# Attention loads in another order and two gate outputs held until 1/rms is spread

## The chip, the cores and the metric

The kernel runs on one core of one Trainium2 chip. The metric is the device time of one execution in microseconds (us). The profile names the engines PE (TensorE matmul), PEld (its weight loads), DVE (VectorE), ACT (ScalarE), POOL (GpSimd) and SP (SyncE, which issues most DMAs).

## The reference

One layer of an encoder for 1024 tokens of width 1024. A combined input projection feeds two groups of heads, a bidirectional mLSTM and a neighbourhood attention over a grid of 16 rows by 64 columns; then come an output projection, an MLP and a gated embedding.

```python
def reference(x, p, norm1_g, w_in, ..., w_ple_gate, w_ple_up):
    u = rms_norm(h, norm1_g[i])
    proj = jnp.einsum('bsd,de->bse', u, w_in[i])
    y_a = mlstm_mixer(mq, mk, mv, mo, mg, ...)
    y_b = neighbourhood_attention(nq, nk, nv, q_norm_g[i], k_norm_g[i], rpb[i])
    h = h + jnp.einsum('bse,ed->bsd', jnp.concatenate([y_a, y_b], axis=-1), w_out[i])
    z = jnp.einsum('bsd,df->bsf', rms_norm(h, norm2_g[i]), w_ff1[i])
    h = h + jnp.einsum('bsf,fd->bsd', jnp.square(jax.nn.relu(z)), w_ff2[i])
    gate = jax.nn.sigmoid(jnp.einsum('bsd,de->bse', rms_norm(h, ple_norm_g[i]), w_ple_gate[i]))
    h = h + gate * jnp.einsum('bsk,kd->bsd', p[i], w_ple_up[i])
```

In the attention each query sees a window of 8 rows by 16 columns; a relative position bias, taken from `rpb`, is added to the scores before the softmax.

## The kernel before

Everything is held transposed, channels on the 128 partitions and the 1024 tokens along the free axis. Products run in three passes of split operands (`passes`: high by high, high by low, low by high). The stages follow each other: input projections, mLSTM by head (`mlstm_front`, `mlstm_sweeps`, `mlstm_finish`), attention with the output projection between its steps, the rest of the output projection, the MLP's two products, the gate.

**Attention.** 32 units n are handled in an order written out by hand (`with tc.manual_schedule()`): a pair of heads (`pr`, 4), a half of the grid (`rb`, 2), a block of columns (`cb`, 4; `KW` gives 24 or 32 key columns). In unit n, PE computes the scores of n+1 and the values (probabilities times `vw`) of n-1; DVE and ACT make the softmax of n+1 (`exps`, which adds the bias table `tab`), ACT and POOL normalise it (`norm`; POOL's half is L955), PE transposes the probabilities of n (`pt`, L966), and DVE and ACT copy them out (`pT`).

Between these steps other work is put. `run(nv1, k)` takes k steps of the last projection (24 matmuls each, evacuated by ACT into `nv1t` with three buffers and written to `nvd` by SP). `y_split` splits the mLSTM's output into a high and a low part. `fill(k)` takes k matmuls (`op`, L1014) of the output projection: six jobs (`JOBS`) of two output rows `e` each, three over the four mLSTM inputs (48 matmuls each), three over three attention inputs (36 each). `FILLA` and `FILLB` give k for each quarter of the 32 units. A job's weights are loaded by `w_raw` (buffers `wr`, three) and split by `w_split` on ACT and DVE; the sums are added to the rows `h` of x that `out_res` loads.

**Tables.** `tab_load(n)` fills a unit's table of 128 partitions: 64 from `tabI` through SP, 64 from `tabU` through POOL's queue, and a strip set to a constant on POOL. Five buffers (`TABS`) let the load of table n+5 start when the softmax of unit n has read its own. The source of each part is a list of dimensions whose outermost has 4 entries:

```python
for q_, tb, p0, r0, c0, nr in ((nc.sync, tabI, io, 0, 0, 12), (nc.gpsimd, tabU, bo, r_0, a0, 8)):
    src = bass.AP(tb.tensor, tb.offset + k0 * 30 * kw + r0 * 2 * kw,
                  [[2 * kw, 4], [30 * kw, 16], [1, nr * 2 * kw]])
```

`load_vw(pr)` loads the values of a pair of heads in four DMAs, one for each `cb`, from `nvd[:, columns, pr]`, whose outermost dimension also has 4 entries. SP issues its DMAs in the order of its list, and each waits for what its buffer waits for. The pool `m2`, which holds tables, values and probabilities, opens when the mLSTM's pool `m1` closes.

**Gate.** For each of eight rows e and two halves t of the tokens `g_unit(e, t)` makes 24 matmuls into a PSUM tile; `g_out` multiplies by 1/rms (`Rb`), takes the sigmoid, multiplies by the embedding and adds. For the first row (e = 0) the sum of squares is finished on PE (`n_1ps`, `n_0ps`), DVE and POOL (`sumsq_to_rstd`; POOL takes the power), and PE transposes and ACT copies spread it (`bcast_rstd`; `n_1R`, `n_0R`). This stage's order is not written out by hand.

Of the kernel before, what the change touches and what calls it, by code (L numbers as in the profile page):

```python
# [11 lines left out]
F32 = mybir.dt.float32  # L12
# [6 lines left out]
P = 128  # L19
# [16 lines left out]
TABS = 5  # L36
PCS = 5
FILLA = (4, 4, 3, 7)
FILLB = (4, 4, 3, 7)
# [5 lines left out]
NEG = -1.0e30  # L45
# [13 lines left out]
def tile_block(ctx, tc, xT, pT, w_in, w_out, w_ff1, w_ff2, w_gate, w_up, vecs, gate_b, rpbp, con,  # L59
               outT, dbg=None):  # L60
    nc = tc.nc
# [617 lines left out]
    aa, MP, wpv, wj, enm = (gk[n] for n in ("aa", "MP", "wpv", "wj", "enm"))  # L679
    m1p_ctx = tc.tile_pool(name="m1p", bufs=1, space=PSUM)  # L680
    m1p = m1p_ctx.__enter__()
    with tc.tile_pool(name="m1", bufs=2) as m1:
# [185 lines left out]
        for h in range(4):  # L868
            mlstm_sweeps(h)
            if h == 0:  # L870
                na_ssq(7)
            if h < 3:
                mlstm_front2(h + 1)
                run(o0) if h == 0 else run(o1, 5) if h == 1 else run(o1)
            if h < 2:
                mlstm_front(h + 2)
            if h == 2:
                nv1 = proj_nv(1)
        run(nv1, NV1)
# [9 lines left out]
    with tc.tile_pool(name="m2", bufs=2) as m2, tc.tile_pool(name="m2p", bufs=2, space=PSUM) as m2p:  # L889
# [10 lines left out]
        NU = 32  # L900
        g3 = lambda t_: t_.rearrange("p (r c) -> p r c", c=64)
        heads2 = (slice(0, 64), slice(64, 128))
        tabs, scs, sms, pts, pvs, vws, ys = {}, {}, {}, {}, {}, {}, {}

        def geom(n):
            pr, u = divmod(n, 8)
            rb, cb = divmod(u, 4)
            return pr, rb, cb, KW[cb], 12 * KW[cb]

        def tab_load(n):  # L910
            if n >= NU:
                return
            pr, rb, cb, kw, w_ = geom(n)
            tab = m2.tile([P, 12, 2, 32], F32, tag="tab", name=f"tab{n}", bufs=TABS)
            tab = tab.rearrange("p a s b -> p (a s b)")[:, : 2 * w_]
            io, bo = (0, 64) if rb == 0 else (64, 0)
            r_0, a0, dead = (4, 0, 8) if rb == 0 else (0, 4, 0)
            k0 = (64 if cb > 1 else 0) + 16 * pr
            for q_, tb, p0, r0, c0, nr in ((nc.sync, tabI, io, 0, 0, 12), (nc.gpsimd, tabU, bo, r_0, a0, 8)):
                tb = tb[min(cb, 3 - cb)]  # L920
                src = bass.AP(tb.tensor, tb.offset + k0 * 30 * kw + r0 * 2 * kw,
                              [[2 * kw, 4], [30 * kw, 16], [1, nr * 2 * kw]])
                q_.dma_start(tab[p0 : p0 + 64, c0 * 2 * kw : (c0 + nr) * 2 * kw], src)
            G.memset(tab[bo : bo + 64, dead * 2 * kw : (dead + 4) * 2 * kw], NEG)
            tabs[n] = tab.rearrange("p (a s b) -> p s a b", s=2, b=kw)
# [119 lines left out]
        raws, ws_ = {}, {}  # L1045

        def fill_jobs():
            for i, (es, ks) in enumerate(JOBS):
                if i + 1 < len(JOBS):
                    raws[i + 1] = w_raw(*JOBS[i + 1])  # L1050
                n = 0
                while len(yhi) <= ks[-1]:
                    yield
                for _ in out_proj(es, ks, mmps, ws_.pop(i)):
                    n += 1
                    if n == 12 and i + 1 < len(JOBS):
                        ws_[i + 1] = w_split(raws.pop(i + 1), *JOBS[i + 1])
                    yield

# [42 lines left out]
        with tc.manual_schedule():  # L1102
            for n in range(TABS):
                tab_load(n)
                if n == 1:
                    vws[0] = load_vw(0)
            raws[0] = w_raw(*JOBS[0])
# [5 lines left out]
            for n in range(NU):  # L1113
# [17 lines left out]
                if n < 4:  # L1131
                    run(nv1, 1 if n < 2 else None)
                    if n > 1:
                        y_split(2 * n - 4)
                else:
                    fill(FILLA[n // 8])
# [11 lines left out]
                if n < 4:  # L1148
                    run(nv1, 1) if n < 2 else None
                    if n > 1:  # L1150
                        y_split(2 * n - 3)
                    if n == 2:
                        ws_[0] = w_split(raws.pop(0), *JOBS[0])
                else:
                    fill(FILLB[n // 8])
                if n in (2, 3, 9):
                    e0 = {2: 0, 3: 2, 9: 4}[n]
                    out_res(e0)
                    out_res(e0 + 1)
# [3 lines left out]
            run(fills)  # L1163
# [170 lines left out]
    with tc.tile_pool(name="ff2", bufs=2) as ff2:  # L1334
# [143 lines left out]
        g_load(2)  # L1478
        for e, t in [(0, 1), (1, 1), (0, 0), (1, 0)] + [(e, t) for e in range(2, 8) for t in (1, 0)]:
            if (e, t) == (7, 0):  # L1480
                parts = [g_unit(e, t, q * 256, 256) for q in range(2)]
                for ps, cs in parts:
                    g_out(e, ps, cs, V)
                continue
            ps, cs = g_unit(e, t)
            if e == 0:
                rs3 = sumsq_to_rstd(acc3[t], hc[t], f"n3_{t}")
                bcast_rstd(rs3, hc[t], f"n3_{t}")
            g_out(e, ps, cs, G if t else V)
            if t == 0 and e + 2 < 8:  # L1490
                g_weights(e + 2)
                load_up(e + 2)
                if e + 3 < 8:
                    g_load(e + 3)
# [53 lines left out]
```

## Time and profile before

| | before |
|---|---|
| median of 3 runs | 1414.97 us (1414.75 to 1416.21) |
| profiled execution | 1421.5 us |
| span of its instructions | 1419.7 us |
| PE busy | 1316.8 us (93%) |
| DVE, ACT, POOL busy | 916.7, 592.8, 566.3 us |
| data moved by DMA | 206.06 MB, mean 145 GB/s |

The profile is of one execution. A row of the chain of waits gives the start, the length and what the last-ending chain of work spent it on; "DMA tab<-tabU" is the time from a DMA's issue to its landing. [...] A tile's buffer numbers are left out of its name.

### The profile page before, as it was taken

How to read it: one execution, taken by the hardware profiler on the slowest of the kernel's cores; microseconds unless marked ns; L12 is line 12 of the kernel's file. 1: busy time of each engine (PE TensorE's matmuls, PEld its weight loads, DVE VectorE, ACT ScalarE, POOL GpSimd, SP SyncE). 2: the span in 40 equal slices, each digit the busy share in tenths (PEclk: the TensorE clock that was granted, in tenths of full speed). 3: DMA queues.
4: the chain of work that ended last, by engine and by line, in shares of the span. 5: the costliest groups of instructions: out<-in, count | busy, mean ns of one | idle time of the engine just before them, and what ended most of it. 6: DMA issues, size and time to landing. Idle time of an engine off the chain costs nothing.

```text
span 1419.7 us, 19398 instructions
## 1 busy us (share of the span) xinstructions
PE 1316.8 (93%) x7115; PEld 1100.4 (78%) x7115; DVE 916.7 (65%) x1419; ACT 592.8 (42%) x971; POOL 566.3 (40%) x456
## 2 busy tenths in 40 slices
PE   7999999999987669997899999999999799999898
PEld 6888777899876447775678888888788578888787
DVE  4487897665662436669856666665638998568433
ACT  7453343455553435545333333323433334455321
POOL 2215675553431112206456555665203560026422
PEclk9999999999998789998899999999999999999999
DMA  8543333564325454411144444455876674452342
GB/s 277 206 145 96 107 119 105 175 216 153 105 72 146 140 138 102 133 45 45 31 163 151 146 153 135 150 163 188 296 261 224 190 227 124 151 155 62 92 138 82
DMA packets 155343, 206.06 MB, mean 145 GB/s; under 512 B 20848, under 2 KB 104880, under 8 KB 155248
## 3 DMA queue, kind: packets, MB, share of 16 engines
q1 hardware_dynamic: 142480, 182.10, 40.7%
q10 hardware_dynamic: 7200, 13.11, 2.8%
q0 software_dynamic: 5568, 9.61, 2.4%
q8 instruction: 56, 0.92, 0.3%
q14 instruction: 39, 0.32, 0.1%
HBM read 151.60 MB, written 53.17 MB: 144 GB/s over the span
## 4 chain that ended last, share of the span: by engine, by line
PE 62%; DVE 7%; DMA 6%; issue 4%; POOL 2%; ACT 1%; SPq 0%; DVEq 0%; POOLq 0%; ACTq 0%
PE f_P L1364 17%; PE p_s_t L255 9%; PE g L1433 6%; PE p L255 6%; PE op L1014 4%; PE p_s L255 3%; PE p_t L255 3%; PE o0p L309 2%; PE pv L986 2%; DMA wo_4r<-w_out 1%; PE o1p L309 1%; PE pt L966 1%; PE num L754 1%; PE sc L936 1%; DMA tab<-tabI 1%
## 5 line engine op out<-in xcount | busy, mean ns | idle before, releaser
L1253 DVE TENSOR_TENSOR zl<-zr,zh 128x1024 fp32r<-128x1024 f32 x56 | 82.4, 1479 | 6.3 <-ACT zh L1252 6.3
L255 PE MATMUL p<-b,w_ah 128*128 128x512 f32 x256 | 80.3, 396 | 3.5 <-DVE b L192 3.5
L955 POOL TENSOR_SCALAR pc<-pc,st 128x288 f32<-128x288 f32 (+1 forms) x32 | 17.2, 538 | 154.6 <-DVE st L950 94.8
L1234 POOL TENSOR_TENSOR w2re<-sk,w2re 128x512 f32<-128x512 f32 x16 | 27.0, 1686 | 100.1 <-issue 63.5
L259 DVE TENSOR_TENSOR z<-z,p_s_t 128x512 f32<-128x512 f32 x64 | 42.5, 685 | 33.0 <-PE p_s_t L255 31.7
L1252 ACT ACTIVATE zh<-zr 128x1024 fp32r<-128x1024 f32 x56 | 58.3, 1047 | 12.0 <-DMA zr<-zd 11.1
L255 PEld LDWEIGHTS p<-b,w_ah 128*128 128x128 f32 x256 | 48.9, 191 | 14.1 <-DVE b L192 3.9
L986 PE MATMUL pv<-pT,vw 128*64 128x128 f32 (+1 forms) x384 | 30.4, 295 | 31.7 <-DVE pT L975 31.7
L1364 PE MATMUL f_P<-zl,w2h 128*128 128x512 f32 x128 | 51.7, 404 | 8.2 <-DVE zl L1253 8.1
L255 PE MATMUL p<-b,w_al 128*128 128x512 f32 x128 | 50.8, 399 | 7.6 <-DVE w_al L140 7.6
L945 ACT ACTIVATE pc<-pc,st 128x288 f32<-128x288 f32 (+1 forms) x64 | 36.3, 569 | 48.7 <-DVE st L944 48.7
L944 DVE CUSTOM_DVE_ANT_1 pc<-sc,tab 128x288 f32<-128x288 f32 (+1 forms) x64 | 29.9, 504 | 40.2 <-POOL pc L955 12.6
L1387 POOL TENSOR_TENSOR h<-h,evP 128x512 f32<-128x512 f32 x8 | 14.8, 1886 | 98.3 <-ACT evP L1378 98.3
L1277 POOL TENSOR_TENSOR tz<-z,z 128x512 f32<-128x512 f32 x16 | 20.8, 1298 | 82.6 <-ACT z L1266 82.6
L986 PEld LDWEIGHTS pv<-pT,vw 128*64 128x64 f32 (+1 forms) x384 | 22.1, 144 | 39.1 <-DVE pT L975 33.1
L1433 PE MATMUL g<-gh,wg_l 128*128 128x512 f32 (+1 forms) x136 | 52.4, 386 | 0.0
L1433 PE MATMUL g<-gh,wg_h 128*128 128x512 f32 (+1 forms) x136 | 52.4, 385 | 0.0
L758 POOL TENSOR_SCALAR wv<-vh,wj 128x129 f32<-128x129 f32 x56 | 30.4, 546 | 54.6 <-PE num L759 49.5
L1433 PE MATMUL g<-gl,wg_h 128*128 128x512 f32 (+1 forms) x136 | 52.0, 382 | 0.0
L1364 PE MATMUL f_P<-zh,w2h 128*128 128x512 f32 x128 | 50.7, 396 | 1.2 <-ACT zh L1252 1.2
L1265 DVE SCALAR_TENSOR_TENSOR z<-z,Rb 128x1024 f32<-128x1024 f32 x32 | 50.5, 1582 | 0.9 <-ACT Rb L179 0.9
L1364 PE MATMUL f_P<-zh,w2l 128*128 128x512 f32 x128 | 50.6, 395 | 0.0
(698 smaller groups left out, 4607.4 us busy)
## 6 DMA issues: line engine op xcount, KB each, us to landing
zr<-zd SPq DMA_DIRECT2D x56, 512.0 KB
zd<-z ACTq DMA_DIRECT2D x48, 256.0 KB
w2r<-w_ff SPq DMA_DIRECT2D x48, 256.0 KB
w_0r<-w_ff SPq DMA_DIRECT2D x16, 512.0 KB
w_1r<-w_ff SPq DMA_DIRECT2D x16, 512.0 KB
zd<-tz SPq DMA_DIRECT2D x32, 256.0 KB
zd<-z SPq DMA_DIRECT2D x32, 256.0 KB
w2re<-w_ff SPq DMA_DIRECT2D x16, 512.0 KB
```

The source lines that it names most:

```text
L255: TE.matmul(ps, x_, y_, start=j == 0 and i == 0, stop=j == 3 and i == 2)
L259: mark["add"] = V.tensor_tensor(o, a, b, op=ALU.add).ins
L309: mm = TE.matmul(ps[:, :256], a, b, start=k == 0 and i == 0, stop=k == KT - 1 and i == 2)
L758: G.tensor_scalar(wv, vh[:, c, 0:129], wj[:, col], 1.0, op0=ALU.mult, op1=ALU.mult)
L945: S.activation(pb, pb, AF.Exp, scale=-1.0, bias=st[:, 0:1], accum_out=st[:, 1:2])
L986: TE.matmul(pv[e0 : e0 + 64, cb], vws[pr][: 4 * kw, cb, rb + j, e0 : e0 + 64], pT[s][: 4 * kw, j], start=j == 0, stop=j == 2)
L1014: TE.matmul(ps, a, b, start=n == 0 and i == 0, stop=n == len(ks) - 1 and i == 2)
L1252: S.activation(hi, raw, AF.Copy)
L1253: dv.append(V.tensor_tensor(lo, raw, hi.bitcast(F32), op=ALU.subtract).ins)
L1265: V.scalar_tensor_tensor(z_, z_, 0.0, Rb, op0=ALU.max, op1=ALU.mult)
L1364: pe_last = TE.matmul(ps[n, e], a, b, start=st and k == 0, stop=sp and k == 2)
L1433: TE.matmul(ps, x_, y_, start=k == 0 and i == 0, stop=k == KT - 1 and i == 2)
```

## The change

`tab0` gets a pool of its own with one buffer, opened ahead of the mLSTM's pools; every fifth table uses it, the others rotate over four buffers. Table 0 is loaded in the mLSTM stage. `tabU` is issued by SP. The last projection takes two, one, one and one steps in units 0 to 3; `y_split` comes once in each of units 3 to 6; the fills start with unit 7 (`NJ`) and take ten a unit at first. A job's weights are loaded when the job two ahead of it is being split (`job_weights`), the first three in units 1, 4 and 6; rows `h` come one a unit in units 4 to 7, 9 and 10. In the gate two outputs are collected in `held` until the transposes of 1/rms have been issued, and weights are loaded one row further ahead.

```diff
-FILLA = (4, 4, 3, 7)
-FILLB = (4, 4, 3, 7)
+FILLA = (5, 5, 4, 7)
+FILLB = (5, 5, 4, 7)
+NJ = 7
...
+    tb0_ctx = tc.tile_pool(name="tb0", bufs=1)
+    tb0 = tb0_ctx.__enter__()
     m1p_ctx = tc.tile_pool(name="m1p", bufs=1, space=PSUM)
...
+        pool, tag, bufs = tabp[0] if n % TABS else (tb0, "tab0", 1)
+        tab = pool.tile([P, 12, 2, 32], F32, tag=tag, name=f"tab{n}", bufs=bufs)
...
+        for q_, tb_, p0, r0, c0, nr in ((nc.sync, tabI, io, 0, 0, 12), (nc.sync, tabU, bo, r_0, a0, 8)):
...
             if h == 2:
                 nv1 = proj_nv(1)
+                tab_load(0)
...
+        tabp.append((m2, "tab", TABS - 1))
...
         def fill_jobs():
             for i, (es, ks) in enumerate(JOBS):
-                if i + 1 < len(JOBS):
-                    raws[i + 1] = w_raw(*JOBS[i + 1])
-                n = 0
                 while len(yhi) <= ks[-1]:
                     yield
+                done[0] = 0
                 for _ in out_proj(es, ks, mmps, ws_.pop(i)):
-                    n += 1
-                    if n == 12 and i + 1 < len(JOBS):
-                        ws_[i + 1] = w_split(raws.pop(i + 1), *JOBS[i + 1])
+                    done[0] += 1
                     yield
+                cur[0] += 1
+
+        def job_weights():
+
+            i = cur[0] + 1
+            if done[0] >= 12 and i in raws and i not in ws_:
+                ws_[i] = w_split(raws.pop(i), *JOBS[i])
+                if i + 2 < len(JOBS):
+                    raws[i + 2] = w_raw(*JOBS[i + 2])
...
-            for n in range(TABS):
+            for n in range(1, TABS):
+                if n == 2:
+                    vws[0] = load_vw(0)
                 tab_load(n)
-                if n == 1:
-                    vws[0] = load_vw(0)
-            raws[0] = w_raw(*JOBS[0])
...
                 if n < 4:
-                    run(nv1, 1 if n < 2 else None)
-                    if n > 1:
-                        y_split(2 * n - 4)
-                else:
+                    run(nv1, 1 if n < 3 else None)
+                if n >= NJ:
                     fill(FILLA[n // 8])
...
-                if n < 4:
-                    run(nv1, 1) if n < 2 else None
-                    if n > 1:
-                        y_split(2 * n - 3)
-                    if n == 2:
-                        ws_[0] = w_split(raws.pop(0), *JOBS[0])
-                else:
+                if n < 1:
+                    run(nv1, 1)
+                if n >= NJ:
                     fill(FILLB[n // 8])
-                if n in (2, 3, 9):
-                    e0 = {2: 0, 3: 2, 9: 4}[n]
-                    out_res(e0)
-                    out_res(e0 + 1)
+                if 3 <= n < 7:
+                    y_split(n - 3)
+                if n == 6:
+                    ws_[0] = w_split(raws.pop(0), *JOBS[0])
+                job_weights()
+                if n in (1, 4, 6):
+                    j = {1: 0, 4: 1, 6: 2}[n]
+                    raws[j] = w_raw(*JOBS[j])
+                if n in (4, 5, 6, 7, 9, 10):
+                    out_res({4: 0, 5: 1, 6: 2, 7: 3, 9: 4, 10: 5}[n])
...
         g_load(2)
+        g_load(3)
+        held = []
...
-            ps, cs = g_unit(e, t)
+            held.append((e, *g_unit(e, t), G if t else V))
             if e == 0:
                 rs3 = sumsq_to_rstd(acc3[t], hc[t], f"n3_{t}")
+                continue
+            if e == 1:
                 bcast_rstd(rs3, hc[t], f"n3_{t}")
-            g_out(e, ps, cs, G if t else V)
-            if t == 0 and e + 2 < 8:
+                if t == 0:
+                    g_weights(2)
+            while held:
+                g_out(*held.pop(0))
+            if e == 1 and t == 0:
+                load_up(2)
+                g_load(4)
+                g_weights(3)
+                load_up(3)
+                g_load(5)
+            elif t == 0 and e + 2 < 8:
                 g_weights(e + 2)
                 load_up(e + 2)
-                if e + 3 < 8:
-                    g_load(e + 3)
+                if e + 4 < 8:
+                    g_load(e + 4)
```

The order of the instructions shows it at three places. First the list of SP from table 5 on: `nv1t` are steps of the last projection, `nr` raw queries and keys, `vw1` the second set of values, `wo0_0r` the first job's weights. Before:

```order
L923 DMA tab4_4403<-tabI0_111 64x1x576
L1020 DMA wo0_0r_4407<-w_out 128x4x256
L923 DMA tab5_4445<-tabI1_112 64x1x768
L342 DMA nvd_81<-nv1t3_4474 128x2x128
L342 DMA nvd_81<-nv1t4_4518 128x2x128
L836 DMA nr3_4536<-qnd3_85 128x1024
L894 DMA vw1_4538<-nvd_81 96x1x512
L894 DMA vw1_4538<-nvd_81 128x1x512 x2
L894 DMA vw1_4538<-nvd_81 96x1x512
L923 DMA tab6_4551<-tabI1_112 64x1x768
```

and now:

```order
L708 DMA tab5_4446<-tabI1_112 64x1x768
L708 DMA tab5_4446<-tabU1_114 64x1x512
L343 DMA nvd_81<-nv1t3_4475 128x2x128
L343 DMA nvd_81<-nv1t4_4519 128x2x128
L866 DMA nr3_4537<-qnd3_85 128x1024
L925 DMA vw1_4539<-nvd_81 96x1x512
L925 DMA vw1_4539<-nvd_81 128x1x512 x2
L925 DMA vw1_4539<-nvd_81 96x1x512
L708 DMA tab6_4552<-tabI1_112 64x1x768
L708 DMA tab6_4552<-tabU1_114 64x1x512
L343 DMA nvd_81<-nv1t5_4581 128x2x128
L1029 DMA wo0_0r_4600<-w_out 128x4x256
```

Each table now has two rows in SP's list, and the first weights stand behind table 6 instead of ahead of table 5. Second, SP's list in the mLSTM stage, where `mq7` and `qw2_0` are loads of that stage. Before:

```order
L149 DMA nv1_0r_3957<-w_in 128x4x256
L690 DMA mq7_3571<-mqd7_105 128x1024
L334 DMA ogd_80<-o0t0_2926 128x256
L707 DMA qw2_0_3136<-Md_110 128x1024
L696 DMA vh2_3131<-vd_79 128x8x128
```

and now:

```order
L150 DMA nv1_0r_3960<-w_in 128x4x256
L708 DMA tab0_3972<-tabI0_111 64x1x576
L708 DMA tab0_3972<-tabU0_113 64x1x384
L720 DMA mq7_3574<-mqd7_105 128x1024
L335 DMA ogd_80<-o0t0_2929 128x256
```

Both parts of table 0 stand there, 35 rows and more ahead of the other tables. Third, PE in the gate, where `g0_1`, `g1_1` and `g0_0` are the first three outputs (row, half), `n3_1ps` the sum of squares and `n3_1R0` the transposes that spread 1/rms. Before:

```order
L1433 MATMUL g0_1_0_11463<-gh7_11419,wg0_l_11430 128x512
L166 MATMUL n3_1ps_11488<-ones_71,acc3_1_11211 128x1 x4
L1433 MATMUL g1_1_0_11509<-gh0_11179,wg1_h_11437 128x512
L1433 MATMUL g1_1_0_11509<-gl0_11180,wg1_h_11437 128x512
L178 MATMUL n3_1R0_11497<-cn_70,n3_1rs_11495 128x128 x4
L1433 MATMUL g1_1_0_11509<-gh0_11179,wg1_l_11438 128x512
```

and now, where the 24 matmuls of `g1_1` follow the sum of squares and end with the first three rows here:

```order
L1448 MATMUL g1_1_0_11503<-gh7_11423,wg1_h_11441 128x512
L1448 MATMUL g1_1_0_11503<-gl7_11424,wg1_h_11441 128x512
L1448 MATMUL g1_1_0_11503<-gh7_11423,wg1_l_11442 128x512
L179 MATMUL n3_1R0_11528<-cn_70,n3_1rs_11501 128x128 x4
L1448 MATMUL g0_0_0_11546<-gh0_11183,wg0_h_11433 128x512
```

The transposes moved from behind the second matmul of `g1_1` to behind its last; those of the other half moved in the same way.

## Rows read from the trace of the kernel before

**Rows 1.** The page: the span, and each engine's busy time.

```profile
span 1419.7 us, 19398 instructions
PE 1316.8 (93%) x7115; PEld 1100.4 (78%) x7115; DVE 916.7 (65%) x1419; ACT 592.8 (42%) x971; POOL 566.3 (40%) x456
```

**Rows 2.** Chain of waits, 395 to 660 us: start us, us, what.

```profile
421.98 7.20 DMA tab<-tabU
...
431.62 0.50 POOL pc L955
...
472.64 12.62 DMA wo_2r<-w_out
...
510.63 17.40 DMA wo_4r<-w_out
...
546.01 0.66 PE pt L966 x6
...
587.13 0.79 PE pt L966 x6
587.92 1.63 PE op L1014 x7
```

**Rows 3.** Waits, 417 to 545 us: waiter, releaser, us in total, times, longest.

```profile
PE pv L986 <- DVE pT L975: 31.4, 4, 13.7
...
ACT wo_4h L137 <- DMA wo_4r<-w_out: 12.8, 1, 12.8
...
ACT wo_2h L137 <- DMA wo_2r<-w_out: 9.5, 1, 9.5
...
PE sc L936 <- DVE st L944: 7.4, 2, 7.3
```

**Rows 4.** By windows: the stretches at clock 0.50 in the attention stage.

```profile
430.12:434.86 4.74, 4.74 (x20) 4.21 (x21) 1.86 (x9) 2.85 (x9) 1.45 (x3) 0.50 0.36 111
...
sum 22.18, PE 22.01 PEld 18.74 DVE 13.01 ACT 9.54 POOL 6.26; mean PE 4.40 PEld 3.75 DVE 2.60 ACT 1.91 POOL 1.25
```

**Rows 5.** By windows, last columns: granted clock, DMA share, GB/s.

```profile
423.00:430.00 7.00, 0.00 (x0) 0.00 (x0) 0.40 (x3) 0.43 (x1) 3.35 (x8) 0.62 0.57 108
423.00:488.00 65.00, 40.18 (x322) 34.70 (x322) 21.88 (x59) 24.78 (x57) 12.04 (x26) 0.83 0.54 155
436.00:438.00 2.00, 2.00 (x19) 2.00 (x19) 0.62 (x2) 1.46 (x3) 0.67 (x2) 1.00 0.26 94
480.00:482.00 2.00, 0.00 (x0) 0.00 (x0) 0.00 (x0) 0.00 (x0) 0.00 (x0) 1.00 0.26 90
486.00:488.00 2.00, 0.00 (x0) 0.00 (x0) 1.62 (x3) 0.95 (x3) 0.00 (x0) 0.50 0.07 26
```

**Rows 6.** DMA issues: tensors, queue, count, KB each, median us to landing.

```profile
tab<-tabI SPq DMA_DIRECT2D x16, 192.0 KB
tab<-tabI SPq DMA_DIRECT2D x16, 144.0 KB
...
tab<-tabU POOLq DMA_DIRECT2D x16, 128.0 KB, 6.3
vw<-nvd SPq DMA_DIRECT2D x8, 256.0 KB
tab<-tabU POOLq DMA_DIRECT2D x16, 96.0 KB, 6.1
vw<-nvd SPq DMA_DIRECT2D x8, 192.0 KB
```

**Rows 7.** Timeline of PE in the gate: the idle time before stands in brackets.

```profile
1326.92 0.48 PE L178 MATMUL n_1R<-cn,n_1rs 128*128 128x128 f32 x1 [2.35 <-POOL n_1rs L170]
...
1343.75 0.32 PE L178 MATMUL n_0R<-cn,n_0rs 128*128 128x128 f32 x1 [1.69 <-POOL n_0rs L170]
```

**Rows 8.** By windows: the gate's stretch at clock 0.50, and one at 1.00.

```profile
1327.00:1332.50 5.50, 5.50 (x15) 4.48 (x16) 0.69 (x1) 2.51 (x3) 1.73 (x2) 0.50 0.00 0
1333.00:1338.00 5.00, 5.00 (x23) 4.13 (x22) 0.69 (x1) 0.63 (x1) 1.61 (x2) 1.00 0.14 52
```

More of the change, by code (lines that the diff above doesn't have):

```diff
@@ L679, in tile_block, with geom, tab_load @@
     aa, MP, wpv, wj, enm = (gk[n] for n in ("aa", "MP", "wpv", "wj", "enm"))
+    tb0_ctx = tc.tile_pool(name="tb0", bufs=1)
+    tb0 = tb0_ctx.__enter__()
     m1p_ctx = tc.tile_pool(name="m1p", bufs=1, space=PSUM)
     m1p = m1p_ctx.__enter__()
+    NU = 32
+    tabs, tabp = {}, []
+    def geom(n):
+        pr, u = divmod(n, 8)
+        rb, cb = divmod(u, 4)
+        return pr, rb, cb, KW[cb], 12 * KW[cb]
+    def tab_load(n):
+        if n >= NU:
+            return
+        pr, rb, cb, kw, w_ = geom(n)
+        pool, tag, bufs = tabp[0] if n % TABS else (tb0, "tab0", 1)
+        tab = pool.tile([P, 12, 2, 32], F32, tag=tag, name=f"tab{n}", bufs=bufs)
+        tab = tab.rearrange("p a s b -> p (a s b)")[:, : 2 * w_]
+        io, bo = (0, 64) if rb == 0 else (64, 0)
+        r_0, a0, dead = (4, 0, 8) if rb == 0 else (0, 4, 0)
+        k0 = (64 if cb > 1 else 0) + 16 * pr
+        for q_, tb_, p0, r0, c0, nr in ((nc.sync, tabI, io, 0, 0, 12), (nc.sync, tabU, bo, r_0, a0, 8)):
+            tb_ = tb_[min(cb, 3 - cb)]
+            src = bass.AP(tb_.tensor, tb_.offset + k0 * 30 * kw + r0 * 2 * kw,
+                          [[2 * kw, 4], [30 * kw, 16], [1, nr * 2 * kw]])
+            q_.dma_start(tab[p0 : p0 + 64, c0 * 2 * kw : (c0 + nr) * 2 * kw], src)
+        G.memset(tab[bo : bo + 64, dead * 2 * kw : (dead + 4) * 2 * kw], NEG)
+        tabs[n] = tab.rearrange("p (a s b) -> p s a b", s=2, b=kw)
     with tc.tile_pool(name="m1", bufs=2) as m1:
@@ L897, in tile_block @@
         hres = {}
-        NU = 32
         g3 = lambda t_: t_.rearrange("p (r c) -> p r c", c=64)
         heads2 = (slice(0, 64), slice(64, 128))
[L903 to L925, printed above, removed]
+        tabp.append((m2, "tab", TABS - 1))
+        scs, sms, pts, pvs, vws, ys = {}, {}, {}, {}, {}, {}
         def scores(n):
@@ L1044, in tile_block @@
         JOBS = [((e, e + 1), ks) for ks in (range(0, 4), range(4, 7)) for e in (0, 2, 4)]
-        raws, ws_ = {}, {}
+        raws, ws_, done, cur = {}, {}, [0], [0]
         def fill_jobs():
             for i, (es, ks) in enumerate(JOBS):
-                if i + 1 < len(JOBS):
-                    raws[i + 1] = w_raw(*JOBS[i + 1])
-                n = 0
                 while len(yhi) <= ks[-1]:
                     yield
+                done[0] = 0
                 for _ in out_proj(es, ks, mmps, ws_.pop(i)):
-                    n += 1
-                    if n == 12 and i + 1 < len(JOBS):
-                        ws_[i + 1] = w_split(raws.pop(i + 1), *JOBS[i + 1])
+                    done[0] += 1
                     yield
+                cur[0] += 1
[5 more added lines that the diff above has]
+                    raws[i + 2] = w_raw(*JOBS[i + 2])
         fills = fill_jobs()
@@ L1162, in tile_block @@
             values_out(NU - 1, True)
-            run(fills)
+            for _ in fills:
+                job_weights()
+    tb0_ctx.__exit__(None, None, None)
     pj_ctx.__exit__(None, None, None)
```

## The prediction

> **What bounds the kernel now.** I read the page first. PE is busy for 93% of the span [rows 1], so only PE's idle time and its stretches at half clock can be saved, and they must lie in the two stages that the change touches. Next I read the chain of waits. In the attention stage it leaves PE for DMAs four times that matter: a table at 421.98 (7.20 us), weights at 472.64 (12.62) and at 510.63 (17.40), and tables in between [rows 2]. The waits of PE between 417 and 545 us say the same from PE's side: it stood for 31.4 us in four waits for the probabilities' copy pT and for 7.4 us in two waits for the softmax [rows 3]. ACT shows who was late behind that: it runs its list in order, and the split of w_out's weights held it for 9.5 and 12.8 us until they had landed [rows 3]. After each long wait the granted clock is 0.50: five such stretches hold 22.0 us of PE work [rows 4], so they cost 11.0 us more. PE's loss in this stage is 38.8 + 11.0 = 49.8 us. That is a ceiling, not the forecast.
>
> Why were those loads late? The windows by DMA share tell it [rows 5]. From 423 to 488 us the DMA engines are never at rest, yet long stretches run at a share of 0.26 and 90 to 94 GB/s: four of sixteen engines work. In these stretches only tables (tabI) and value tiles (vw) are left in the SP queue. Both are read with a source whose outermost dimension is 4 in the code, while with wide loads among them the same 65 us have a mean of 155 GB/s. So tables and values use four engines only, wide loads leave a quarter of their bytes on the same four, and a wide load lands only when that quarter has passed the tables ahead of it. At 486 to 488 us this backlog runs dry [rows 5], as the first wait for weights ends. I call its content the four-engine ledger. In KB, tabI has 192 or 144, tabU 128 or 96, a vw set 2 x 256 + 2 x 192 = 896 [rows 6]; of a 512 KB load 128 count.
>
> **What rate do the four engines have?** Quiet: 94 GB/s [rows 5], which is 91.8 KB per us with the issue table's KB of 1024 bytes. Under load: between 423 and 488 us the ledger of the kernel before is tables 0 to 11 (6 x 192 + 6 x 144 = 2016), two vw sets (1792), and quarters of two w_out loads, two nr, four h and five nvd writes (256 + 256 + 512 + 160): 4992 KB in 65 us, 76.8 KB per us. In its first 7 us the POOL queue's five tabU competed (108 GB/s at a share of 0.57, more than four engines) and only tables 0 and 1 passed, 336 KB. Without that, 4656 KB in 58 us are 80.3. The change leaves the POOL queue out of this stage, so I take the middle between 80.3 and 91.8, 86, and keep 76.8 and 91.8 as ends.
>
> **The change part by part: attention.** The list of orders moves four things. (a) tab0 is loaded in the mLSTM stage, before its space was free in the kernel before: the first wait (7.27 of the 7.4 us) goes. (b) w_out's weights are loaded two jobs ahead, at units 1, 4, 6, and h rows come one per unit: the waits of 9.5 and 12.8 us of ACT lose their cause. (c) The last five steps of nv1, the y_splits and the fills are moved between units; no PE work is added. The fills start at unit 7 with ten per unit, so they end by unit 22. Edits to y_split, the weights' split and out_res cost nothing by themselves, since DVE and ACT wait for PE or DMA in this stage [rows 3]. (d) tabU goes from POOL's queue to SP's. POOL loses 32 issues that nobody waited for. SP gains 32 issues; its own list is not the bound, but what stands behind them (vw, weights, h, nr) is delayed with the tables. tabU has the same source pattern as tabI, so I let it run on the same four engines: 128 or 96 KB per unit more on the resource that was already busy from 423 to 488. No row shows tabU on SP; the bounds are that all of it falls there and that a quarter does (as for a wide load).
>
> [...]
>
> Now the ledger of the changed kernel, from 423 us to the landing of table 24 (the last before the fills of seven, which PE bounds in either kernel): tables 1 to 24 are 12 x 320 + 12 x 240 = 6720 KB; four vw sets 3584; quarters of six nr and six h loads 1536; of three w_out loads of 512 KB and three of 384 KB 384 + 288; of five nvd writes 160. Together 12672 KB. At 86 KB per us that is 147.3 us, so table 24 lands at 570.3. From a landing to the transposes: the first table landed at 429.18 (421.98 + 7.20), POOL's normalisation ended at 432.12, some 3 us [rows 2]. So unit 24's transposes come at 573.3 instead of 587.13 [rows 2]: 13.8 us earlier. At 91.8 it is 564.0 (23.1 earlier), at 76.8 it is 591.0 (3.9 later).
>
> Does PE allow it? By the same ledger 8224 KB stand up to table 14: 423 + 95.6 + 3 = 521.6 for unit 14's transposes, which were at 546.01. From there to unit 24 PE took 41.1 us [rows 2]; nine more fills at 1.63/7 = 0.233 us [rows 2] make 43.2: 565 us. PE is ready first, so the tables set the end. PE then stands elsewhere than before: around unit 5 (table 6 is behind the second vw set: 3744 KB, 466.5 us) and unit 13 (table 14 behind the third).
>
> **The gate.** Before, the transposes that spread 1/rms stood two matmuls behind the sum of squares and waited for POOL: 2.35 and 1.69 us [rows 7]. The first wait was followed by 5.50 us at clock 0.50 [rows 8], which cost 2.7. In the change 24 matmuls (5.00 us for 23 at full clock [rows 8]) lie between, and the transposes needed 2.35 us more: covered. Between 4.0 (if the clock falls anyway) and 6.7 us are saved; I take 6, nearer to the upper end, because nothing else in that stretch stops PE. New waits: two outputs are held, so their PSUM tiles live one unit longer, and the two pools have eight such tiles; ACT's split of wg3 waits for the end of the fourth unit, ahead of the copy of 1/rms, and delays four output chains by about 1 us with no PE behind them. The table loads of the gate change by one issue: nothing.
>
> **Sum.** -13.8 - 6 = -19.8 us against the profiled execution of 1421.5 us (span 1419.7 [rows 1]); I subtract it from the median of 1414.97: **1395**.
>
> **Rivals.** *PE sets the pace* (the intended result): tabU spreads over all engines or the four run at their quiet rate with slack, the 49.8 us go but for the first softmax (1.1 us), gate -6: 1360. For it speaks that weights and rows no longer come in bursts; against it that the ledger at 91.8 already ends at 564. *Slower*: the four engines do worse than in the kernel before, because two loads per table are queued one behind the other and every vw set (896 KB) delays a table that is one unit from use. It decides below 74.6 KB per us, where unit 24's transposes come 8.8 us later than before, the gate's 6 and 0.2% together. At 70 it gives 423 + 181 + 3 = 607, 20 us later, less 6: 1429. For it speaks the rate of 48 in the first 7 us, against it that the POOL queue's competition is gone. *Only the gate counts*: at 79 the stage ends where it did, 1409; it lies inside the forecast's range.
>
> **How the numbers follow.** A difference under 0.2% (2.8 us) is no change in a measurement of this kernel. The tables pace the stage, forecast 1395, own range 1385 (91.8 and -6.7) to 1415 (76.8 and -4): 0.68. PE sets the pace, 1360 to 1385: 0.14. Slower, 1418 to 1435: 0.08. Something that I don't see, half of it faster: 0.10. Faster: 0.68 x 0.95 + 0.14 + 0.05 = 0.84; slower 0.09; same 0.07. The range leaves out the fastest half of the PE case and the slowest cases: 1372 to 1413.
>
> **What would show it.** Right: no wait of ACT for w_out; a DMA share near 0.26 or above without a break from 423 to 560; DVE waiting for tables at units 5 to 6 and 13; unit 24's transposes near 573; no PE gap before the spreads of 1/rms and no half clock there. Wrong: PE without gaps from 423 on (then tabU did not cost the four engines), or ACT still waiting for weights or for the landing of nvd writes.

## The result, and the profile after

The changed kernel takes 1396.97 us (median of 4 runs, 1394.46 to 1398.95) against 1415.59 for the kernel before: a ratio of 0.9863, 95% interval 0.9839 to 0.9886. The forecast was 1395, within 1372 to 1413. The size is right; the rest of this document asks whether the reasons are.

The page of the changed kernel: the span, and each engine's busy time (the rows to compare are [rows 1]).

```profile
span 1397.1 us, 19354 instructions
PE 1321.2 (95%) x7115; PEld 1105.5 (79%) x7115; DVE 914.1 (65%) x1419; ACT 591.5 (42%) x971; POOL 545.7 (39%) x424
```

The span falls by 22.6 us, while PE is busy 4.4 us longer: idle time went, and more of PE's work ran at half clock (31.8 us of it in the attention stage, against 22.0 [rows 4]).

The chain of waits of the changed kernel in the attention stage (start us, us, what) answers to [rows 2]:

```profile
426.16 0.52 SPq L708
...
430.09 12.72 DMA tab<-tabI
442.88 10.85 DMA nvd<-nv1t
...
458.78 12.80 DMA wo_0r<-w_out
471.66 10.23 DMA tab<-tabI
...
511.35 13.67 DMA nr<-qnd
...
525.12 0.75 DVE nr L847
...
526.45 0.55 DVE pT L984
...
531.02 1.12 PE pt L975 x6
...
554.03 15.20 DMA tab<-tabU
...
576.41 0.79 PE pt L975 x6
```

The stage's first load of tabU, for table 1, leaves SP at 426.16 (its tabI 0.6 us earlier). After that the chain still goes from DMA to DMA, of every kind that SP's queue carries, up to table 23, which lands at 554.03 + 15.20 = 569.23. Two of these links are no waits for data. The nvd write at 442.88 leaves when the tabI load of 430.09 has landed (442.81), and the tabI load at 471.66 when wo_0r has (458.78 + 12.80 = 471.58); each stands eight places behind the load that it waited for. All of SP's list shows it: of its 99 DMAs between 417 and 577 us each signals on the semaphore of the one eight places ahead of it, none leaves before that one has landed, and 56 leave within 0.1 us of that landing. So here a load of SP waited, besides for its buffer, for the landing of the one eight places ahead. Unit 24's transposes stand at 576.41 instead of 587.13. ACT's waits no longer contain w_out at all (it was 9.5 and 12.8 us [rows 3]), and PE's waits for pT, 31.4 us before [rows 3], are 5.6 us. The waits of PE in the changed kernel, 417 to 577 us (waiter, releaser, us in total, times, longest):

```profile
PE sc L945 <- DVE st L953: 6.0, 5, 2.6
PE pv L995 <- DVE pT L984: 5.6, 5, 2.8
PE pv L995 <- DVE yl L1010: 2.4, 1, 2.4
```

The windows by DMA share (span, then per engine busy and count, granted clock, busy share of the 16 DMA engines that the page counts, GB/s), as in [rows 5]:

```profile
436.00:438.00 2.00, 2.00 (x19) 1.87 (x19) 0.00 (x0) 0.23 (x1) 0.13 (x1) 1.00 0.26 100
450.00:452.00 2.00, 2.00 (x18) 2.00 (x18) 0.00 (x0) 0.00 (x0) 0.00 (x0) 1.00 0.25 87
560.00:562.00 2.00, 2.00 (x15) 1.42 (x13) 1.21 (x3) 1.58 (x4) 0.87 (x2) 1.00 0.25 91
504.00:506.00 2.00, 2.00 (x24) 1.70 (x21) 0.37 (x2) 1.15 (x4) 0.00 (x0) 1.00 0.26 98
```

With tabU in SP's queue the share does not fall below 0.25 from 430 us on, in windows of 2 us, and comes back to 0.25 or 0.26 wherever no wide load is in flight: the work of four of the 16 engines, all the time, though PE works. That is what the ledger said.

DVE's timeline shows when tables land: a softmax whose idle time (in brackets) a table ended. Counted from the start, these rows are units 2, 6 and 14, and unit 25 in a later stretch:

```profile
444.18 0.56 DVE L953 CUSTOM_DVE_ANT_1 pc<-sc,tab 128x384 f32<-128x384 f32 x1 [8.98 <-DMA tab<-tabU]
...
470.00 0.56 DVE L953 CUSTOM_DVE_ANT_1 pc<-sc,tab 128x384 f32<-128x384 f32 x1 [0.21 <-DMA tab<-tabU]
...
522.44 0.56 DVE L953 CUSTOM_DVE_ANT_1 pc<-sc,tab 128x384 f32<-128x384 f32 x1 [5.45 <-DMA tab<-tabU]
...
575.96 0.56 DVE L953 CUSTOM_DVE_ANT_1 pc<-sc,tab 128x384 f32<-128x384 f32 x1 [0.64 <-DMA tab<-tabU]
```

By the ledger 1536 KB stand up to table 2 (tables 1 and 2 and a vw set), 3744 up to table 6, 8224 up to table 14, and 12672 + 320 = 12992 up to table 25. Divided by the time since 426.16 these are 85, 85, 85 and 87 KB per us: one rate for the whole stage. I had taken 86.

The gate, as in [rows 7, 8]: PE's timeline without idle time ahead of either spread, and the window over both at full clock.

```profile
1313.91 0.60 PE L179 MATMUL n_1R<-cn,n_1rs 128*128 128x128 f32 x4
...
1326.21 0.60 PE L179 MATMUL n_0R<-cn,n_0rs 128*128 128x128 f32 x4
```

```profile
1307.00:1327.00 20.00, 20.00 (x101) 16.79 (x101) 4.91 (x7) 5.54 (x7) 11.29 (x9) 1.00 0.26 79
```

**What was chance in the two profiles.** Up to unit 24 the changed kernel is 10.7 us ahead, although it came 4.1 us late into the stage. Between there and the gate it gains another 4.8 us, where nothing changed. Both are chance, as the kernel with the gate's part alone (first experiment) shows: its other stages are those of before, and it too comes late into the stage and is early at the gate. Over all the profiles the entry scatters by some 6 us, with the change and without; from unit 24 to the gate's sum of squares the profiled execution of before takes 736.0 us, the others 731.2 to 734.3. PE's timeline, the first y transposes and the gate's first sum of squares, of before:

```profile
418.86 1.11 PE L791 MATMUL py<-cn,hh 128*128 128x128 f32 x4 [0.30 <-DVE hh L790]
...
1323.04 0.95 PE L166 MATMUL n_1ps<-ones,acc 128*128 128x1 f32 x8
```

The same of the kernel with the gate's part alone, with the spread:

```profile
422.32 1.12 PE L791 MATMUL py<-cn,hh 128*128 128x128 f32 x4 [0.30 <-DVE hh L790]
...
1319.40 0.95 PE L166 MATMUL n_1ps<-ones,acc 128*128 128x1 f32 x8
...
1325.79 0.60 PE L178 MATMUL n_1R<-cn,n_1rs 128*128 128x128 f32 x4
```

So of the 22.6 us between the profiles 10.7 + 4.1 = 14.8 are the attention stage and 22.6 - 10.7 - 4.8 = 7.1 the gate; 4.1 lost and 4.8 gained are noise that nearly cancels. The attention stage isn't free of it either: the kernel with the gate's part alone, 3.5 us late at its entry, is only 0.6 us late at unit 24 (587.7), so some 3 of the 14.8 us may be the profiled execution of before.

### The profile page after: what moved, and what is told of

Same layout as the page of the kernel before. It is cut to its first block, busy times and chain, and to the rows that moved or that the text cites. A ratio compares the mean times of both kernels' runs of the same rounds, so it can differ in the third digit from the quotient of the medians.

```text
span 1397.1 us, 19354 instructions
## 1 busy us (share of the span) xinstructions
PE 1321.2 (95%) x7115; PEld 1105.5 (79%) x7115; DVE 914.1 (65%) x1419; ACT 591.5 (42%) x971; POOL 545.7 (39%) x424
## 4 chain that ended last, share of the span: by engine, by line
PE 56%; DMA 6%; DVE 6%; issue 3%; POOL 1%; ACT 1%; SPq 1%; DVEq 0%; POOLq 0%; ACTq 0%
PE f_P L1379 19%; PE p_s_t L256 9%; PE g L1448 6%; PE p L256 6%; PE op L1023 3%; PE p_s L256 3%; PE p_t L256 3%; DMA tab<-tabI 2%; PE pv L995 1%; DMA tab<-tabU 1%; PE o1p L310 1%; DMA nr<-qnd 1%; DMA wo_0r<-w_out 1%; DVE h L1025 1%; PE pt L975 1%
## 5 line engine op out<-in xcount | busy, mean ns | idle before, releaser
L256 PE MATMUL p<-b,w_ah 128*128 128x512 f32 x256 | 80.3, 395 | 4.2 <-DVE b L193 4.2
L964 POOL TENSOR_SCALAR pc<-pc,st 128x288 f32<-128x288 f32 (+1 forms) x32 | 17.5, 548 | 160.9 <-DVE st L959 143.8
L1267 ACT ACTIVATE zh<-zr 128x1024 fp32r<-128x1024 f32 x56 | 58.5, 1048 | 12.8 <-DMA zr<-zd 11.9
L1402 POOL TENSOR_TENSOR h<-h,evP 128x512 f32<-128x512 f32 x8 | 14.8, 1886 | 98.3 <-ACT evP L1393 98.3
L138 ACT ACTIVATE w_bh<-w_0r 128x1024 fp32r<-128x1024 f32 x16 | 17.0, 1063 | 73.0 <-POOL w_0r L234 53.3
L138 ACT ACTIVATE w_ah<-w_0r 128x1024 fp32r<-128x1024 f32 x16 | 17.0, 1061 | 68.4 <-PE p_t L256 68.4
```

The lines of the kernel that those rows point to most:

```text
L138: mark["hi"] = S.activation(hi, raw, AF.Copy).ins
L256: TE.matmul(ps, x_, y_, start=j == 0 and i == 0, stop=j == 3 and i == 2)
L1267: S.activation(hi, raw, AF.Copy)
```

## The experiments

The theory is the ledger: tables and value tiles run on the same four DMA engines, and their content decides when tables land. Its rivals: the order of the loads alone made and cured the waits; the queue (POOL's against SP's) matters by itself; or the number of loads or all bytes count. Each ratio is to runs of the kernel before that were made beside it, whose medians lie between 1415.4 and 1419.2 us.

| kernel | median us | ratio to before | 95% interval |
|---|---|---|---|
| changed | 1396.97 | 0.9863 | 0.9839 to 0.9886 |
| gate alone | 1410.69 | 0.9973 | 0.9945 to 1.0 |
| all but the gate | 1401.38 | 0.989 | 0.9854 to 0.9927 |
| changed, tabU in POOL's queue | 1385.17 | 0.9786 | 0.9749 to 0.9823 |
| changed, tables with 16 outermost | 1381.67 | 0.9752 | 0.9722 to 0.9783 |
| the same, tabU in POOL's queue | 1382.33 | 0.9745 | 0.9713 to 0.9778 |
| before, tabU in SP's queue | 1422.15 | 1.0031 | 1.0013 to 1.0048 |
| before, tables with 16 outermost | 1398.85 | 0.9859 | 0.9824 to 0.9893 |
| changed, vw loads cut in four | 1393.45 | 0.9829 | 0.9791 to 0.9868 |
| changed, table 0 meant to be late | 1399.1 | 0.987 | 0.9837 to 0.9904 |
| changed, dose with 4 outermost | 1422.11 | 1.0032 | 1.0012 to 1.0053 |
| changed, dose with 16 outermost | 1409.06 | 0.994 | 0.9918 to 0.9961 |
| changed, dose of 2 KB loads | 1404.86 | 0.9912 | 0.9885 to 0.9939 |

**The two parts apart.** The gate's block of the diff put into the kernel before, and taken out of the changed one.

> The kernel before with the gate's part of the change alone. The traces put 7.07 us of the gain into the gate, so 1415.6 - 7 = 1408.5, and no PE wait for the 1/rms row and no half clock there. Rival (the gate's gain in the trace of the changed kernel is chance of that execution): 1412 to 1416.

> The changed kernel with the gate's part undone. If the parts add, 1397 + 7 = 1404, and the attention stage is as in the changed kernel (unit 24's transposes near 576). Rival (the 4.8 us that the changed kernel gains between the attention stage and the gate belong to neither part and are chance of one execution): the sum of this gain and of the gate's alone then falls short of the whole gain by some us in the traces, but not in the medians.

Measured: 1410.69 and 1401.38. The trace of the gate's part alone has its spread without idle time (row above), and its span of 1409.0 us is 10.7 below that of before, 3.6 of them ahead of the gate: 7.1 us for the gate, as in the changed kernel. The medians put it at 4.7 and 4.4 us; the interval of the first reaches up to 1.0. Both traces were set against the same execution of before, and the other traces tell why the figures differ. In the kernel with all but the gate's part, the gate's sum of squares begins at

```profile
1303.16 0.95 PE L167 MATMUL n_1ps<-ones,acc 128*128 128x1 f32 x8
```

and the span is 1397.2 us, so from there to the end the gate takes 94.0 us. In the other profiles without the gate's part it is 96.7 us (before), 95.6 (before, tabU in SP's queue) and 96.9 (before, tables with 16 outermost); in all ten with it, 89.6. The part is worth 4.4 to 7.3 us, 6.2 on average, by how badly the old gate happened to go. The parts add: the attention stage is worth 14.0 us by medians, and 14.0 + 4.7 is the whole gain. Unit 24's transposes in that kernel come at 570.9, not near 576; it entered the stage 3.4 us earlier than the changed kernel. The 4.8 us between the stages are chance.

**The queue undone.**

```
-  for ... in ((nc.sync, tabI, io, 0, 0, 12), (nc.sync, tabU, bo, r_0, a0, 8)):
+  for ... in ((nc.sync, tabI, io, 0, 0, 12), (nc.gpsimd, tabU, bo, r_0, a0, 8)):
```

> The changed kernel with one part undone: tabU is loaded again by POOL's queue. Ledger theory (four fixed engines carry tabI, tabU and vw, and their content sets when the tables land): 2688 of the 12672 KB up to table 24 leave the four engines, so table 24 lands at about 426 + 124 = 550 us, before PE wants it; PE sets the pace, unit 24's transposes come at 563 to 570 instead of 576.3, and the kernel takes 1378 to 1391 us, faster than the changed kernel's 1397. Rival (it was POOL's queue that made the kernel before slow, by its issues or by competition with SP's loads): the time goes back towards the kernel before, 1400 to 1412.

Measured: 1385.17, and unit 24's transposes in PE's timeline at

```profile
568.52 0.86 PE L975 MATMUL pt<-cn,pc 128*96 128x128 f32 x6
```

The move of tabU to SP's queue costs the changed kernel 12 us; without that line the change would have been worth 30 instead of 19. The rival that POOL's queue was the trouble is gone: by it this kernel would have been slower than the changed one. Which engines carry tabU in POOL's queue no row shows; the DMA share in the four windows above is 0.46, 0.36, 0.90 and 0.35 here instead of 0.25 and 0.26.

**The same tables with 16 outermost.** The query order within a unit is turned from (row, column) to (column, row) within each half of the partitions, so that the source can run 16 columns in its outermost dimension (wide, where one with 4 outermost is narrow):

```
-  [[2 * kw, 4], [30 * kw, 16], [1, nr * 2 * kw]])
+  [[30 * kw, 16], [2 * kw, 4], [1, nr * 2 * kw]])
-  uo = lambda t_: t_.rearrange("p c (r i) -> p c r i", i=16)
+  uo = lambda t_: t_.rearrange("p c (h i r) -> p c h r i", h=2, i=16)
```

> The changed kernel with the same tables loaded through a source whose outermost dimension is 16 instead of 4 (the query order within a unit is turned so that it fits; same bytes, same queue, same place of every issue). Ledger theory: the tables leave three quarters of their bytes to the other engines, 7632 KB stay on the four up to table 24, they are done by about 520 us, and PE sets the pace: no stretch at a DMA share of 0.26, transposes of unit 24 at 560 to 570, 1375 to 1390 us. Rival (the pace is set by the order of the loads and by the softmax's chain, not by four engines): within 3 us of the changed kernel's 1397.

> The changed kernel with the tables read through an outermost dimension of 16 and tabU in POOL's queue. With the narrow source, tabU in SP's queue cost 12 us against POOL's queue (1397 against 1385). Ledger theory: that cost was the four engines; with tables over all engines the queue makes no difference: 1379 to 1385, as the kernel with wide tables in SP's queue (1381.7). Rival (the 12 us were the number of loads in SP's list, whatever the engines): another several us faster, 1370 to 1377. Second rival (POOL's queue disturbs SP's loads): 1387 or more.

Measured: 1381.67, and 1382.33 with tabU in POOL's queue. With wide tables in SP's queue, the windows of the stretches shown above, and one longer:

```profile
436.00:438.00 2.00, 2.00 (x18) 1.88 (x16) 0.00 (x0) 0.24 (x1) 0.47 (x2) 1.00 0.39 122
450.00:452.00 2.00, 2.00 (x27) 1.83 (x23) 1.00 (x4) 1.17 (x5) 0.00 (x0) 1.00 0.76 213
504.00:506.00 2.00, 2.00 (x13) 1.41 (x11) 1.21 (x3) 1.88 (x5) 0.55 (x1) 1.00 0.46 153
560.00:562.00 2.00, 2.00 (x23) 1.39 (x23) 0.81 (x4) 0.43 (x1) 0.33 (x2) 1.00 0.41 142
504.00:520.00 16.00, 16.00 (x129) 12.42 (x128) 10.96 (x31) 9.57 (x23) 2.43 (x6) 1.00 0.22 64
```

and the transposes of units 14 and 24 in PE's timeline:

```profile
514.25 0.82 PE L975 MATMUL pt<-cn,pc 128*128 128x128 f32 x6
...
558.14 0.86 PE L975 MATMUL pt<-cn,pc 128*96 128x128 f32 x6
```

Same bytes, same queue, same places of issue; beside the turned query order only the outermost dimension differs, and 15 us go. The queue that cost 12 us with narrow tables costs nothing with wide ones (1381.67 against 1382.33). So the queue's cost was that of narrow tables in it, and not of more loads in SP's list. The semaphores in the traces tell narrow loads from wide ones: in the changed kernel, between 417 and 577 us, each of SP's 72 loads of tabI, tabU and vw raises its semaphore in 5 steps, each of its 20 of nr, h and w_out in 16; with the turned source the tables take 16 and vw stays at 5.

In the changed kernel the share is 0.25 to 0.26 where narrow loads are alone, the work of four of 16 engines; which four they are no row shows. The share alone would not prove it: with wide tables it falls to 0.22 between 504 and 520, but with 64 GB/s, where the narrow stretches have 87 to 100. The expectation of no such stretch was too simple, and the transposes came 1.9 us ahead of its range.

**Either half of the cure on the kernel before.** Its tabU moved to SP's queue, or its tables' source turned, and nothing else.

> The kernel before with tabU moved to SP's queue and nothing else. Ledger theory: 1344 KB more on the four engines up to table 11, so the weights of the first two jobs land later, by up to 15.6 us at 86 KB per us less what POOL's loads cost them before: 1418 to 1432 us, ACT's waits for w_out longer than 9.5 and 12.8 us. Rival (POOL's queue cost the kernel before its time): faster than before by some us.

> The kernel before with nothing changed but the tables' source order (outermost dimension 16, for tabI in SP's queue and tabU in POOL's). Ledger theory: from 423 to 488 us 3300 instead of 4992 KB on the four engines, so the first weights land near 465 instead of 488 and PE's long waits mostly go: 1382 to 1397 us without any of the reordering. Rival (the order of the loads made the waits): ACT still waits for w_out, 1405 to 1415.

Measured: 1422.15 and 1398.85. The queue alone loses, in the expected range but with little of the expected mechanism: ACT's waits for w_out in that kernel are

```profile
ACT wo_4h L137 <- DMA wo_4r<-w_out: 12.1, 1, 12.1
ACT wo_2h L137 <- DMA wo_2r<-w_out: 9.9, 1, 9.9
```

one longer, one shorter than before. Its profiled execution is no longer than that of before (1417.9 us against 1419.7), so the trace can't tell how the loss of 0.3% comes about; I leave it open. Wide tables alone gain 18 us, just past the top of the expected range: the wait for wo_2r is gone, a part of the other is left. With the order unchanged that part stands, so the order of the loads was probably a cause too:

```profile
ACT wo_4h L137 <- DMA wo_4r<-w_out: 8.3, 1, 8.3
```

**A dose of bytes.** Behind each of the tables 5 to 24 two more loads into a tile nobody reads; the twin has 16 outermost, the third has 16 outermost and 8 elements instead of 8 * kw in each run.

```
+  if 5 <= n < 25:
+      xt = tabp[0][0].tile([P, 256], F32, tag="xt", name=f"xt{n}", bufs=1)
+      for i in range(2):
+          nc.sync.dma_start(xt[64 * i : 64 * i + 64, : 8 * kw], bass.AP(tb_.tensor,
+              tb_.offset + k0 * 30 * kw, [[2 * kw, 4], [30 * kw, 16], [1, 8 * kw]]))
```

> The changed kernel with a dose of extra bytes on the four engines: behind each of the tables 5 to 24 two more loads of 64 or 48 KB (each a part of a table) into a tile that nobody reads, with a source whose outermost dimension is 4. 2128 KB more stand ahead of table 24; at 86 KB per us that is 24.7 us: unit 24's transposes near 601, and 1397 + 25 = 1422 us (1416 to 1428). Rival (what counts is the number of loads in SP's queue or the bytes in all): the same time as its twin with the dose spread over all engines.

> The twin: the same extra bytes in the same number of loads at the same places, but with a source whose outermost dimension is 16. Ledger theory: a quarter of the dose, 532 KB, stands on the four engines: 6.2 us, 1403 us (1399 to 1408). Rival (number of loads or bytes in all count): as its twin, within 4 us.

> The kernel with the dose over all engines, but with 2 KB in each of the added loads: same number of loads, same places, same waits for the tile, hardly any bytes. The dose over all engines cost 12 us where the ledger gave 6.2. If the bytes did all of it, 1397 to 1399; if the number of loads and their waits in SP's list did the other 6, 1402 to 1405.

Measured: 1422.11, 1409.06 and 1404.86: the first and the third in their ranges, the twin 1 us above its own. (The doses ahead of table 24 add up to 2144 KB, not 2128.) DVE's timeline of the kernel with the narrow dose, units 2, 14 and 25:

```profile
440.48 0.56 DVE L958 CUSTOM_DVE_ANT_1 pc<-sc,tab 128x384 f32<-128x384 f32 x1 [10.10 <-DMA tab<-tabU]
...
530.94 0.56 DVE L958 CUSTOM_DVE_ANT_1 pc<-sc,tab 128x384 f32<-128x384 f32 x1 [2.98 <-DMA tab<-tabU]
...
597.91 0.56 DVE L958 CUSTOM_DVE_ANT_1 pc<-sc,tab 128x384 f32<-128x384 f32 x1 [1.86 <-DMA tab<-tabU]
```

From table 2 to table 14 it takes 90.46 us instead of 78.26, 12.2 more for the 1024 KB of doses 5 to 13; to table 25 it takes 157.43 instead of 131.78, 25.65 more for 2240 KB. That is 84 and 87 KB per us, the ledger's rate again. The two other doses cost more than their bytes: loads of 2 KB cost 8 us. The waits of SP's queue there (417 to 590 us) point to a reason:

```profile
SPq L712 <- DMA xt<-tabU: 31.7, 14, 5.7
```

The extra tile has one buffer, so SP's list stood until an earlier load into it had landed, 31.7 us in 14 times, and all later loads started later. The added loads also stand in the list in which each load of the changed kernel waited for the one eight places ahead (above); a run with more buffers, which would tell the two apart, was not made. With narrow doses these waits were 50.6 us in 18 times (417 to 600 us), yet the rate stayed at 84 to 87 KB per us; that they were hidden there behind work already queued is my estimate. That would be why the difference of the twins, 13 us, is less than the ledger's 24.7 - 6.2 = 18.5: the twin paid in SP's list. The rival, equal times, is refuted by those 13 us; that loads cost something besides bytes is shown too.

**The value tiles spread.**

```
-  nc.sync.dma_start(vw[0 : 4 * KW[cb], cb], nvd[:, KC0[cb] : KC0[cb] + KW[cb], pr])
+  for a in range(4):
+      nc.sync.dma_start(vw[a * KW[cb] : (a + 1) * KW[cb], cb], nvd[a, KC0[cb] : KC0[cb] + KW[cb], pr])
```

> The changed kernel with the value tiles spread instead of the tables: each vw load is cut into four, whose outermost dimension is 32 or 24 keys instead of 4 rows (48 loads more in SP's queue, same bytes). If a load of 24 goes over 12 engines and one of 32 over 16, a vw set leaves about 256 instead of 896 KB on the four engines, 2560 KB less up to table 24: it lands near 426 + 118 = 544 us, and PE sets the pace: unit 24's transposes at 563 to 570, 1380 to 1391 us, like the kernel with tabU in POOL's queue. Rival (the tables themselves are slow, or the number of loads in the queue counts): 1394 or more.

Measured: 1393.45, 2.5 us above the range, just short of the rival's 1394 and 8 above the kernel with tabU in POOL's queue. Unit 24's transposes in its trace:

```profile
570.72 0.86 PE L976 MATMUL pt<-cn,pc 128*96 128x128 f32 x6
```

In the stage it does nearly what was expected (0.7 us behind the range, 5.7 ahead of the changed kernel). By their semaphores the loads did spread: those of 24 keys raise theirs in 13 steps and those of 32 keys in 16, where each vw load took 5; that they ran on 12 and 16 engines no run shows. The 48 loads more were not priced. SP's vw loads waited longer for tables to land (417 to 590 us) here, in the first row, than in the changed kernel, in the second:

```profile
SPq L926 <- DMA tab<-tabI: 13.5, 8, 2.8
```

```profile
SPq L925 <- DMA tab<-tabI: 5.2, 4, 1.7
```

That these waits are behind the 8 us is not shown; what the loads cost I did not measure apart.

**Table 0 late.** Its load written at the start of the attention stage.

> The changed kernel with table 0 loaded at the start of the attention stage instead of in the stage before. Ledger theory: 320 KB more in the stage, 3.7 us: 1400.7 (1399 to 1403), although PE waits for the first softmax by 6 to 7 us more. Rival (the first wait comes on top of all): 1403 to 1405. Second rival (hidden): 1397.

Measured: 1399.1, with a spread of 1394 to 1403. But the edit did not do what it was meant to. In SP's timeline of this kernel table 0 still leaves in the mLSTM stage,

```profile
309.89 0.67 SPq L708 DMA_DIRECT2D tab<-tabI  x1
```

where the changed kernel has it at 308.25; its tile lies in the pool that opens ahead of that stage. PE's wait for the first softmax is 0.66 us, as in the changed kernel. So the run is in effect the changed kernel once more, and tests none of the three values; what the early table 0 is worth stays open.

## Why the prediction was right, point by point

**The waits for w_out and the first softmax go.** Right: no wait of ACT for w_out is left, and PE's wait for the first softmax fell from 7.27 to 0.65 us. What the early table 0 is worth for the whole, no run shows. PE's timeline of before and, behind it, of the changed kernel:

```profile
430.12 1.06 PE L936 MATMUL sc<-kh,q 64*128 64x384 f32 x2 [7.27 <-DVE st L944]
```

```profile
428.03 1.06 PE L945 MATMUL sc<-kh,q 64*128 64x384 f32 x2 [0.65 <-DVE st L953]
```

**tabU falls on the same four engines.** Right as far as the runs show it, and the step that decided the size. The rows of before showed the share for tabI and vw only; tabU on SP's queue was argued. With tabU in the queue the share is again 0.25 to 0.26 where no wide load is in flight, tabU raises its semaphore in 5 steps as tabI and vw do, and the queue undone and the wide tables were worth 12 and 15 us. Which engines carry a load no row shows, nor that a wide load leaves just a quarter of its bytes on the four, as the ledger assumes; with these quarters counted its rate came out the same at four landings. But SP's own list was less free than I had written: its table loads stood 15.0 us, in 11 waits between 423 and 577, for tabI loads to land.

**86 KB per us.** Right: 85 to 87 at four landings, and 84 and 87 for the dose. That it was the middle of 80.3 and 91.8 was luck: nothing had decided between these two, and they put table 24 nearly 20 us apart.

**Table 24 at 570.3, its transposes at 573.3.** The transposes came at 576.4. The ledger began 3.2 us later than I had put it (426.16 instead of 423), because this execution came late into the stage; with that, table 14 is due at 521.8 and DVE got it at 522.44, and table 24 is due at 573.5. DVE's timeline has unit 24's softmax without idle time ahead of it, 2.9 us before the transposes:

```profile
573.48 0.45 DVE L953 CUSTOM_DVE_ANT_1 pc<-sc,tab 128x288 f32<-128x288 f32 x1
```

The step that was mis-sized is the 3 us from a landing to the transposes, for unit 14. I had read them up to the end of the normalisation, and behind it other work can stand. Unit 14's transposes came at 530.8 instead of 521.6, 8.4 us behind its table: the rows nr, issued at 511.35, landed only at 525.02, and DVE handles them ahead of the copy pT that PE needed (chain above). So PE was not ready for unit 24 at 565. From unit 14 to unit 24 it took 45.5 us, and with wide tables 43.9 (558.14 - 514.25; I had 43.2): there the tables still cost it 1.6 us. At that pace, an estimate, it would have come to unit 24 at 574.7 without them. The end was thus set mostly by what had landed up to unit 14, and only at the last by the tables behind it; that the sum through table 24 alone came out so close is partly luck. (The fills do not end by unit 22, as I had written; PE's fills of seven go on behind unit 24. The nine more between units 14 and 24 are right, and the sum used only those.) Against its own entry into the stage the gain is 14.8 us, some of it noise (above), forecast 13.8; by medians it is 14.0.

**The gate, 6 us.** Right: 4.4 to 7.3 us by the profiles, 6.2 on average; 4.4 and 4.7 in medians. The 7.1 of two traces, above my upper end of 6.7, rests on one execution of before. The mechanism is as told: no idle time ahead of the spreads, and a granted clock of 1.00 from 1307 to 1327 us.

**What to look for.** Right: no w_out wait, the share, the gate. Table 14 stopped DVE for 5.45 us as foreseen, table 6 only for 0.21; the longest wait, 8.98 us for table 2 behind the first vw set, was not on the list although the same ledger gives it. One sign that I had named against the theory did appear: ACT still waited for the landing of an nvd write, 5.4 us against 4.1 before. I had taken it for a rival's mark wrongly: by the ledger, which counted a quarter of such a write (32 of 128 KB), it stands behind the tables too.

**Not foreseen: the clock.** The stretches at clock 0.50 of the changed kernel, by windows:

```profile
467.00:487.48 20.48, 17.86 (x91) 13.61 (x92) 11.73 (x29) 11.18 (x25) 2.59 (x7) 0.50 0.57 174
...
sum 37.55, PE 31.76 PEld 25.28 DVE 19.14 ACT 19.06 POOL 5.49; mean PE 7.94 PEld 6.32 DVE 4.79 ACT 4.77 POOL 1.37
```

31.8 us of PE work at half clock instead of 22.0 [rows 4], so 15.9 instead of 11.0 us lost, an estimate by the clock (in the gate of before one of these matmuls, 512 wide, follows the other by 0.43 us at 0.50 and by 0.23 at 1.00). PE's longest wait between 417 and 577 us was 2.8 us, where before it was 13.7 [rows 3]. What the half clock cost here no run separates. With wide tables the same sum is

```profile
sum 17.07, PE 16.01 PEld 13.39 DVE 8.60 ACT 9.94 POOL 1.82; mean PE 5.34 PEld 4.46 DVE 2.87 ACT 3.31 POOL 0.61
```

**The rivals.** *PE sets the pace* is what the kernels with wide tables show, but at 1382, not 1360: PE still loses 8.0 us to the clock there and waits some times for DVE and ACT. In the forecast's terms PE would have been ready for unit 24 at 565; it was there at 558.1. *Slower* needed under 74.6 KB per us; the rate never came near it. *Only the gate counts* needed 79.

## What to carry to other kernels

Before a transfer is moved to another queue, write down every load in flight with its source's outermost dimension, and sum the bytes of the narrow ones and, as the ledger assumed, a quarter of the wide ones'; that sum over 86 KB per us, a rate between the quiet stretch's 91.8 and the loaded one's 80.3, gave each of the four landings here within 1.3 us. At the quiet rate the last would have been 8 us off. A DMA share that sat at 0.25 to 0.26 while SP's queue was full was the sign. Turning the source's outermost dimension was worth as much on the kernel before (18 us) as the whole change (19), and another 15 us on top of it. With the dose of 2 KB loads, a load into a buffer that was still being filled held up all loads behind it in SP's list, for 31.7 us in 14 times.

## What the runs showed that I had not expected

Loads of 2 KB, two per table, made the kernel 8 us slower, with 31.7 us of waits for their own tile in SP's list, in 14 times. In the changed kernel none of SP's DMAs between 417 and 577 us left before the one eight places ahead had landed, so a narrow load, which took 5.0 to 17.5 us to land there (12 in the median), held up loads of any kind: the load of nr at 445.50 left 0.02 us behind the landing of a tabI load. And the kernel with wide tables (1381.67) beats both kernels by 34 and 15 us without a byte or a load less.
